# Scheduling edges that bind the casts and low parts of the MLP slabs' weights to the order of their jobs

## The chip, the cores and the metric

The kernel runs on one core of one Trainium2 chip. The metric is the device time of one execution in microseconds, taken as the median of several executions. Beside it there is a profiled execution, whose trace tells when each instruction of each engine ran. Engines are named as in the profile: PE is the matrix engine (TensorE), PEld its weight loads, DVE the vector engine, ACT the scalar engine, POOL the GpSimd engine, and SP the queue that issues most transfers.

## The reference

Two layers of a decoder trunk on 256 tokens of width 2048, in float32. What matters here is the MLP at the end of each layer, whose two weight matrices are 2048 x 8192 and 8192 x 2048:

```python
def squared_relu_mlp(h, w1, w2):
    z = jax.nn.relu(h @ w1)
    return (z * z) @ w2

for i in range(DEPTH):            # DEPTH = 2
    ...
    x = x + jnp.concatenate([token_out, mem_out], axis=-1) @ w_out[i]
    x = x + squared_relu_mlp(rms_norm(x, ffn_norm[i]), w_ff1[i], w_ff2[i])
```

The output is x, 1 x 256 x 2048.

## The kernel before

**Weights in two parts.** Every weight is loaded as float32 and split into a high part, which is a cast to the reduced type fp32r on ACT (line 176, `hi_ring`), and a low part, which is the weight minus its high part, on DVE (line 179, `lo_ring`). Each product is then three matmuls: high weight by high and low part of the activation, low weight by high part. Both rings have 6 slots of 512 columns. A slot is taken when the split is written down and given back when the matmuls that read it have been written down, so a cast can run only after the matmuls that read its slots before.

**Two streams of jobs share the rings.** `Feed` serves them in one written order, found in a dry run of the whole program (`Plan.close`):

- Plain quads ("N", m): four 128x128 blocks, one slot, cast from a tile `raw`. In the MLP they feed the up tiles (`up_tile`, products into `x_bank`).
- Slabs ("S", n, j): the second MLP matrix is multiplied in a scheme with seven products in place of eight on 2 x 2 blocks. Each layer has 56 slabs, numbered 0 to 55 in layer 0 and 56 to 111 in layer 1; a slab has four jobs. A job is written here as (n,j). Job 0 casts two slots from the tile `slab` (128x1024), job 1 one slot from `slab` (128x512), jobs 2 and 3 two slots each from the tile `room` (128x1024). Their products go into the banks `p`, with activations from `z` or from the sums `sit`.

**What a slab's jobs do beside the split** (`_prepare`). After job 0 the left half of the slab tile is no longer needed as it was, and POOL issues a transfer that adds other weights onto it (`add_right`, line 151); job 1 casts that sum. The same happens after job 2 for job 3, in `room`. Ahead of job 1 stands a step "K": an addition on DVE (line 201) that makes the first half of what job 2 casts; after job 2 another one (line 215) makes the half that job 3 adds onto.

**The order of the jobs** is written by hand (lines 1036 to 1041): for each p the jobs (p+1,0), (p,1), (p,2), (p-1,3). So around slab 50 the written order is

```
(51,0) K50 (50,1) (50,2) (49,3) | (52,0) K51 (51,1) (51,2) (50,3)
```

Between them stand up tiles and their quads; each job has a due time in units of up tiles (`tiles_at`). From slab 50 on the jobs stand further apart, since they are to last to the end of the second part of the MLP. `fill` writes the splits down three steps ahead of the job that reads them, if slots are free.

**After each up tile** its bank is copied by ACT to `room` (line 757), its halves are added (DVE, line 816), then come relu and square on ACT (820, 828), the cast to `z` (768) and its low part (772), the four differences for `sit` on DVE (789 to 792), and their cast and low part (797, 800).

**What sets the order on an engine.** Each engine runs its instructions in one order, fixed when the program is built. The builder starts from the written order and lets an instruction go ahead of an earlier one where, by its own estimate of times, the earlier one is not ready yet. `Feed.order` (line 153) adds an edge between two instructions that binds this choice alone and makes no semaphore. It is used before the change for a few pairs, among them each K step, which comes after the low part of the slab job written last (`last_low`, line 202).

Of the kernel before, what the change touches and what calls it, by code (L numbers as in the profile page):

```python
# [55 lines left out]
class Plan:  # L56
# [7 lines left out]
    def __init__(self):  # L64
        self.entries = []
        self.npos = 0
        self.jobs = []
        self.slabs = []
# [32 lines left out]
class Feed:  # L101


    def __init__(self, tc, wst, wpool, rows, plan, dry):
        self.tc, self.nc, self.wst, self.wpool, self.rows = tc, tc.nc, wst, wpool, rows
        self.plan, self.dry = plan, dry
        self.pos = 0
        self.slab_no = 0
        self.lp = self.pp = 0
        self.raw = {}  # L110
        self.split = {}
        self.second = None
        self.second_of = [None] * 3
        self.loads_ahead = LOADS
        self.behind = None
        self.cast_behind = []
        self.gate = None
        if not dry:
            self.hi = wpool.tile([P, SLOTS * 512], F32R, name="hi_ring")
            self.lo = wpool.tile([P, SLOTS * 512], F32R, name="lo_ring")  # L120
            self.busy = [False] * SLOTS
            self.at = 0
# [48 lines left out]
    def _split(self, job, src, n):  # L171
        a = self._slots(n)
        if a is None:
            return False
        hi, lo = self.hi[:, a * 512 : (a + n) * 512], self.lo[:, a * 512 : (a + n) * 512]
        self.last_cast = self.nc.scalar.copy(hi, src)  # L176
        if self.cast_behind:
            self.order(self.last_cast, self.cast_behind.pop())
        low = self.nc.vector.tensor_sub(lo, src, hi.bitcast(F32))  # L179
        if job[0] == "S":  # L180
            self.last_low = low
        if self.behind:
            self.order(low, self.behind)
            self.behind = None
        self.split[job] = (hi, lo, range(a, a + n))
        return True
# [1474 lines left out]
```

## Time and profile before

| | |
|---|---|
| median of 3 runs | 2005.38 us (2004.85 to 2005.83) |
| the profiled execution's own time | 2004.53 us |
| its span, first to last instruction | 2002.8 us |
| mean granted clock of PE | 0.999 |
| bytes moved by DMA | 420.10 MB, mean 210 GB/s |
| cast of a plain quad, ACT line 176 | 620 ns, 1001 of them |
| low part of a plain quad, DVE line 179 | 694 ns, 1001 of them |
| cast of a two-slot job from `room`, ACT | 1054 ns, 224 of them |
| low part of a two-slot job from `room`, DVE | 1222 ns, 224 of them |
| cast and low part from `slab` (two shapes), mean | 830 and 954 ns, 224 of each |
| accumulating transfers issued by POOL | 224, 256 KB each, median 5.8 us (`room`) and 6.6 us (`slab`) from issue to landing |

The profile's page gives each engine's busy time and the costliest groups of instructions. A row of the timeline has the start in us from the span's start, the duration, engine, line, operation, the names written and read with their shapes, the count of merged instructions, and in brackets the idle time of the engine before it with what ended that. The view of waits sums such idle times by the waiting group and its releaser. Matmuls are pipelined: consecutive ones overlap in the trace, so what counts is the step from start to start. Busy shares are averages over the whole span; what an edit is worth is read at the place where the engine that sets the end stands still.

### The profile page before, as it was taken

To read this page: it belongs to the slowest core of one execution; us is meant where nothing else is said; L and a number is where in the kernel's file an instruction comes from. 1 tells how busy PE (TensorE), PEld (TensorE's weight loads), DVE (VectorE), ACT (ScalarE), POOL (GpSimd) and SP (SyncE) were. 2 spreads that over 40 slices of the span, in tenths; PEclk is the share of its full clock that TensorE was granted. 3 is DMA by queue.
4 is the path that set the end of the run, shared out by engine and by line. 5 is a ranking of instruction groups with operands and counts; after the bars stand their busy time and mean duration, and the time that the engine had idled before them with its cause. 6 is when DMAs were issued, how large, how long until landed. Compare 5 with 4: busy or idle time off the path is not lost.

```text
span 2002.8 us, 32056 instructions
## 1 busy us (share of the span) xinstructions
PE 1993.9 (100%) x10534; PEld 1705.1 (85%) x10534; DVE 1716.2 (86%) x3089; ACT 1498.4 (75%) x2791; POOL 247.0 (12%) x291
## 2 busy tenths in 40 slices
PE   9999999999999999999999999999999999999999
PEld 8888888888888888888888888888888888888788
DVE  8888878889989899899765798878889899899887
ACT  7765577787887878778665699567787878878775
POOL 0001311111111111110000000311111111111110
PEclk9999999999999999999999999999999999999999
DMA  9566567888888888765675534567888888888774
GB/s 318 174 192 192 188 202 208 228 224 234 233 231 227 221 231 230 220 190 179 193 227 192 171 122 150 196 189 214 218 225 227 234 235 226 230 223 228 203 219 145
DMA packets 142727, 420.10 MB, mean 210 GB/s; under 512 B 16096, under 2 KB 18784, under 8 KB 142560
## 3 DMA queue, kind: packets, MB, share of 16 engines
q1 hardware_dynamic: 110160, 359.32, 55.4%
q0 software_dynamic: 32256, 58.73, 17.3%
q8 instruction: 82, 1.34, 0.3%
q14 instruction: 85, 0.70, 0.1%
q10 hardware_dynamic: 144, 0.01, 0.0%
HBM read 415.90 MB, written 2.10 MB: 209 GB/s over the span
## 4 chain that ended last, share of the span: by engine, by line
PE 82%; issue 14%; POOL 3%; DMA 1%; ACT 1%; DVE 1%; POOLq 0%; DVEq 0%; ACTq 0%
PE x_bank L430 19%; PE x_bank L432 9%; PE p L863 6%; PE p L865 6%; PE p L866 6%; PE wo L430 6%; PE wo L432 3%; PE u L430 2%; PE ff L430 2%; POOL room L151 1%; POOL slab L151 1%; PE u L432 1%; PE q L464 1%; PE q L466 1%; PE k L464 1%
## 5 line engine op out<-in xcount | busy, mean ns | idle before, releaser
L176 ACT CAST hi_ring<-raw 128x512 fp32r<-128x512 f32 x1001 | 613.2, 620 | 270.4 <-PE x_bank L430 67.8
L179 DVE TENSOR_TENSOR lo_ring<-raw,hi_ring 128x512 fp32r<-128x512 f32 x1001 | 685.7, 694 | 122.7 <-ACT hi_ring L176 107.2
L430 PE MATMUL x_bank<-fx,hi_ring 128*128 128x512 f32 x1952 | 611.1, 394 | 0.0
L432 PEld LDWEIGHTS x_bank<-fx,lo_ring 128*128 128x128 f32 x1952 | 367.0, 188 | 83.8
L432 PE MATMUL x_bank<-fx,lo_ring 128*128 128x256 f32 x1952 | 383.7, 278 | 0.0
L430 PEld LDWEIGHTS x_bank<-fx,hi_ring 128*128 128x128 f32 x1952 | 320.3, 189 | 24.4 <-ACT room L757 0.3
L176 ACT CAST hi_ring<-room 128x1024 fp32r<-128x1024 f32 x224 | 236.0, 1054 | 126.5 <-PE p L865 105.9
L179 DVE TENSOR_TENSOR lo_ring<-room,hi_ring 128x1024 fp32r<-128x1024 f32 x224 | 273.8, 1222 | 37.3 <-ACT hi_ring L176 28.5
L179 DVE TENSOR_TENSOR lo_ring<-slab,hi_ring 128x512 fp32r<-128x512 f32 (+1 forms) x224 | 213.7, 954 | 59.3 <-ACT hi_ring L176 58.5
L176 ACT CAST hi_ring<-slab 128x512 fp32r<-128x512 f32 (+1 forms) x224 | 186.0, 830 | 47.6 <-PE p L865 23.9
L863 PE MATMUL p<-hi_ring,sit 128*128 128x512 f32 x448 | 176.0, 393 | 1.6 <-ACT hi_ring L176 1.5
L866 PE MATMUL p<-lo_ring,sit 128*128 128x512 f32 x448 | 174.8, 390 | 1.8 <-DVE lo_ring L179 1.8
L865 PE MATMUL p<-hi_ring,sit 128*128 128x512 f32 x448 | 175.4, 391 | 0.0
L151 POOL DMA_DIRECT2D room<-in_w x112 | 96.9, 865 | 563.3 <-DVE lo_ring L179 451.0
L151 POOL DMA_DIRECT2D slab<-in_w x112 | 97.1, 867 | 527.9 <-DVE lo_ring L179 520.0
L430 PE MATMUL wo<-cat,hi_ring 128*128 128x512 f32 x512 | 161.8, 397 | 0.3 <-DVE rc L401 0.3
L863 PE MATMUL p<-hi_ring,z 128*128 128x512 f32 x336 | 132.1, 393 | 0.0
L865 PE MATMUL p<-hi_ring,z 128*128 128x512 f32 x336 | 131.2, 390 | 0.0
L866 PE MATMUL p<-lo_ring,z 128*128 128x512 f32 x336 | 130.8, 389 | 0.0
L432 PEld LDWEIGHTS wo<-cat,lo_ring 128*128 128x128 f32 x512 | 95.9, 188 | 22.0
L866 PEld LDWEIGHTS p<-lo_ring,sit 128*128 128x128 f32 x448 | 84.3, 188 | 21.3 <-DVE lo_ring L179 2.7
L432 PE MATMUL wo<-cat,lo_ring 128*128 128x256 f32 x512 | 101.5, 279 | 0.0
(375 smaller groups left out, 3369.4 us busy)
## 6 DMA issues: line engine op xcount, KB each, us to landing
raw<-in_w SPq DMA_DIRECT2D x500, 512.0 KB, 4.5
slab<-in_w SPq DMA_DIRECT2D x112, 512.0 KB, 4.7
room<-in_w SPq DMA_DIRECT2D x112, 256.0 KB, 4.7
slab<-in_w POOLq DMA_DIRECT2D x112, 256.0 KB, 6.6
room<-in_w POOLq DMA_DIRECT2D x112, 256.0 KB, 5.8
memraw<-in_mem SPq DMA_DIRECT2D x5, 512.0 KB, 4.5
resid<-in_x SPq DMA_DIRECT2D x8, 256.0 KB, 5.3
out_y<-resid SPq DMA_DIRECT2D x16, 128.0 KB, 1.9
```

The costliest lines, as they stand in the source:

```text
L151: self.nc.gpsimd.dma_start(t, self.wst[h, :, 0:512], accum_op=ALU.add)
L176: self.last_cast = self.nc.scalar.copy(hi, src)
L179: low = self.nc.vector.tensor_sub(lo, src, hi.bitcast(F32))
L430: nc.tensor.matmul(ps, hi, xs[:, k, :], start=first and c == 0, stop=False)
L432: nc.tensor.matmul(ps[:, T : 2 * T], lo, xs[:, k, 0:T], start=False, stop=last and c == len(ks) - 1,)
L464: nc.tensor.matmul(ps[t], x[t][1], hi, start=k == 0, stop=False)
L466: nc.tensor.matmul(ps[t], x[t][0], lo, start=False, stop=k == NK - 1)
L863: nc.tensor.matmul(ps, a[1], hi, start=new, stop=False, **again)
L865: nc.tensor.matmul(ps, a[0], hi, start=False, stop=False, **again)
L866: nc.tensor.matmul(ps, a[0], lo, start=False, stop=end, **again)
```

## The change

Each slab job's cast gets an edge to the cast of the slab job written before it, and each slab job's low part an edge to the low part before it. The first slab job has none. Plain quads get no edge, and nothing is added to, or taken from, the instructions themselves.

```diff
@@ -114,6 +114,7 @@
         self.loads_ahead = LOADS
         self.behind = None
         self.cast_behind = []
+        self.last_s = self.last_low = None
         self.gate = None
@@ -178,7 +179,10 @@
             self.order(self.last_cast, self.cast_behind.pop())
         low = self.nc.vector.tensor_sub(lo, src, hi.bitcast(F32))
         if job[0] == "S":
-            self.last_low = low
+            if self.last_low is not None:
+                self.order(self.last_cast, self.last_s.ins.name)
+                self.order(low, self.last_low.ins.name)
+            self.last_s, self.last_low = self.last_cast, low
         if self.behind:
             self.order(low, self.behind)
             self.behind = None
```

## The prediction

> **What bounds the kernel now.** I read the page first, then the waits summed by engine, then the timeline around the longest of them.
>
> ```profile
> span 2002.8 us, 32056 instructions
> ...
> PE 1993.9 (100%) x10534; PEld 1705.1 (85%) x10534; DVE 1716.2 (86%) x3089; ACT 1498.4 (75%) x2791; POOL 247.0 (12%) x291
> ```
>
> TensorE has work in the array for all but 8.9 us, so a change to the casts (ACT) and low parts (DVE) can only pay where TensorE waits for them. The view of waits, for PE alone (total us, times, longest), says where:
>
> ```profile
> PE p L866 <- DVE lo_ring L179: 1.8, 2, 0.9
> PE p L863 <- ACT hi_ring L176: 1.5, 1, 1.5
> PE warm L371 <- PEq L1634: 0.8, 1, 0.8
> PE st_mq L625 <- DVE mq_y L326: 0.3, 1, 0.3
> PE wo L430 <- DVE rc L401: 0.3, 1, 0.3
> ```
>
> 3.3 of these 4.7 us are waits of slab products (p) for a high or low part of their weights. The same view for ACT holds one row in which a cast waits for a slab's transfer:
>
> ```profile
> ACT hi_ring L176 <- DMA slab<-in_w: 8.8, 2, 5.1
> ```
>
> Two times, 3.7 and 5.1 us. The first is in layer 0; rows of the timeline (start, duration, idle before in brackets), thinned:
>
> ```profile
> 814.61 0.86 POOL L151 DMA_DIRECT2D slab<-in_w  x1 [2.62 <-DVE lo_ring L179]
> ...
> 816.00 0.62 ACT L176 CAST hi_ring<-slab 128x512 fp32r<-128x512 f32 x1
> ...
> 816.64 0.42 DVE L816 TENSOR_TENSOR room<-room 128x256 f32<-128x256 f32 x1
> ...
> 817.58 0.68 DVE L201 TENSOR_TENSOR room<-slab,room 128x512 f32<-128x512 f32 x1
> ...
> 818.67 0.63 PE L430 MATMUL x_bank<-fx,hi_ring 128*128 128x512 f32 x2
> ...
> 820.31 0.62 ACT L176 CAST hi_ring<-slab 128x512 fp32r<-128x512 f32 x1 [3.69 <-DMA slab<-in_w]
> ...
> 820.84 0.41 ACT L820 ACTIVATE room<-room 128x256 f32<-128x256 f32 x1
> ...
> 822.04 1.04 ACT L176 CAST hi_ring<-room 128x1024 fp32r<-128x1024 f32 x1
> ...
> 822.62 0.39 PE L866 MATMUL p<-lo_ring,sit 128*128 128x512 f32 x1
> ...
> 823.14 0.50 PE L863 MATMUL p<-hi_ring,sit 128*128 128x512 f32 x1
> ...
> 823.52 1.22 DVE L179 TENSOR_TENSOR lo_ring<-room,hi_ring 128x1024 fp32r<-128x1024 f32 x1
> ...
> 824.79 0.50 PE L866 MATMUL p<-lo_ring,sit 128*128 128x512 f32 x1 [0.92 <-DVE lo_ring L179]
> ...
> 825.13 0.39 PE L863 MATMUL p<-hi_ring,sit 128*128 128x512 f32 x1
> ...
> 826.20 1.05 ACT L176 CAST hi_ring<-room 128x1024 fp32r<-128x1024 f32 x1
> ```
>
> The shapes tell the jobs apart: job 0 casts 128x1024 from slab, job 1 128x512 from slab, jobs 2 and 3 128x1024 from room. The code writes ..., (50,1), (50,2), (49,3), (52,0), (51,1), .... The trace has slab 512 (816.00), slab 512 (820.31), room (822.04), room (826.20), slab 1024 (830.09, below): the cast of job (51,1) runs ahead of three casts written before it. It reads the half to which POOL's transfer of 814.61 adds, so ACT stands until that lands at 820.3, and behind it in ACT's queue stand relu, square and z cast (from 820.84) and the cast of (50,2), which TensorE needs next. Comparing written with run order over all 448 slab casts and 448 low parts, this place and its twin one layer later are the only inversions among them. The twin:
>
> ```profile
> 1892.25 0.62 ACT L176 CAST hi_ring<-slab 128x512 fp32r<-128x512 f32 x1 [5.10 <-DMA slab<-in_w]
> ...
> 1893.17 0.39 PE L866 MATMUL p<-lo_ring,sit 128*128 128x512 f32 x1
> 1895.07 0.50 PE L863 MATMUL p<-hi_ring,sit 128*128 128x512 f32 x1 [1.51 <-ACT hi_ring L176]
> ...
> 1896.73 0.53 PE L866 MATMUL p<-lo_ring,sit 128*128 128x512 f32 x1 [0.92 <-DVE lo_ring L179]
> 1897.06 0.62 PE L863 MATMUL p<-hi_ring,sit 128*128 128x512 f32 x1
> ```
>
> **The change part by part.** Of the 447 edges of each kind, those between neighbours that already stand in order move nothing: all but two. These two put the casts and low parts of (51,1) and (107,1) behind those of (52,0) and (108,0). No instruction, byte or semaphore is added.
>
> *What goes.* The undisturbed step between slab products is 0.225 us (834.25 to 834.70 below is two steps). Layer 0: 822.62 to 825.13 is four steps, 2.51 - 0.90 = 1.61 us lost. Layer 1: 1893.17 to 1897.06, 3.89 - 0.90 = 2.99 us. Then the windows (PE busy and count, PEld, DVE, ACT, POOL, granted clock, DMA share, GB/s):
>
> ```profile
> 825.13:827.11 1.98, 1.98 (x11) 1.48 (x9) 1.98 (x4) 1.98 (x4) 0.77 (x1) 1.00 0.50 33
> 1893.17:1897.06 3.89, 1.46 (x5) 0.59 (x4) 3.17 (x7) 3.28 (x7) 0.09 (x1) 1.00 0.00 0
> 1897.06:1900.47 3.41, 3.41 (x10) 2.75 (x9) 3.41 (x7) 2.34 (x5) 0.77 (x1) 0.50 0.46 122
> ```
>
> After the longer stall the granted clock is 0.50 for 3.41 us; the same stretch of the program took 1.98 us in layer 0 at 1.00, so 1.43 us more. Together 1.61 + 2.99 + 1.43 = 6.03 us.
>
> [...]
>
> *Does (50,2) come in time without it?* Its addend (L201) is done at 818.26. Its two ring slots, worked out from the ring's order, were last read by the matmuls of 818.67 and the low ones right behind: free at 819.30 and 819.53. Relu, square and z cast need the add of 816.64, done at 817.06, and 1.2 us of ACT (820.84 to 822.04): done at 818.3. So its cast runs 819.34 to 820.4 and its low part (1.22) to 821.6. TensorE wants them at 822.85 and 823.30: 2.4 and 1.7 us to spare. In layer 1 the spacing is the same. POOL's next accumulating transfer (after that low part) and SP's loads go earlier with it; both queues keep their order.
>
> *What (51,1) costs in its new place.* Its cast (0.62) and low part (0.68) now follow (52,0):
>
> ```profile
> 830.09 1.05 ACT L176 CAST hi_ring<-slab 128x1024 fp32r<-128x1024 f32 x1
> 831.05 1.14 ACT L176 CAST hi_ring<-raw 128x512 fp32r<-128x512 f32 x2
> 832.85 0.62 ACT L176 CAST hi_ring<-raw 128x512 fp32r<-128x512 f32 x1 [0.66 <-PE x_bank L430]
> ...
> 831.18 1.23 DVE L179 TENSOR_TENSOR lo_ring<-slab,hi_ring 128x1024 fp32r<-128x1024 f32 x1 [0.41 <-ACT hi_ring L176]
> 832.32 0.68 DVE L201 TENSOR_TENSOR room<-slab,room 128x512 f32<-128x512 f32 x1
> 832.92 2.49 DVE L179 TENSOR_TENSOR lo_ring<-raw,hi_ring 128x512 fp32r<-128x512 f32 x4
> ...
> 834.25 0.39 PE L863 MATMUL p<-hi_ring,sit 128*128 128x512 f32 x1
> ...
> 834.70 0.39 PE L866 MATMUL p<-lo_ring,sit 128*128 128x512 f32 x1
> ...
> 1903.48 1.05 ACT L176 CAST hi_ring<-slab 128x1024 fp32r<-128x1024 f32 x1 [1.52 <-PE x_bank L430]
> ```
>
> By its slot, (51,1) is first read at 834.25 (high) and 834.70 (low). The cast of (52,0) waits for TensorE to leave its slots (the last row, its twin in layer 1, tells it), so this stretch keeps its spacing and moves earlier as a whole. Placed right after (52,0), the cast ends at 831.8; the low part, behind the sum of L201, ends at 833.7, 1.0 us early. Queued behind them are the casts and low parts of two plain quads; on ACT the 0.66 us of idle before 832.85 takes the 0.62. If the builder puts all four plain low parts ahead, it ends at 836.0, 1.3 us late. So 0 to 1.3 us a layer; I take 0, because (51,1) is written ahead of those four quads. Its transfer landed at 820.3 and can't bind. DVE has the room:
>
> ```profile
> 818.86:840.00 21.14, 20.09 (x105) 16.44 (x105) 17.17 (x31) 15.84 (x28) 2.60 (x3) 1.00 0.69 199
> ```
>
> 17.17 us of DVE work (third pair) in 21.14, or in 19.53 without the 1.61: 88%.
>
> *Sum.* 2004.53 for the profiled execution less 6.03 is 1998.50. The median of the runs stands 0.85 above that execution, so 1999.35, call it **1999.4**. Were all of the 0.85 stall too, 1998.5; were 0.5 us of stall left at each place, 2000.4.
>
> **The rivals.**
> [...]
> - *A new wait at the new place:* (51,1) comes late by up to 1.3 us a layer, 1999.4 + 2.6 = 2002.0. For it: DVE's four low parts in a row at 832.92; against it: written order and 1.0 us to spare.
> - *Another reader of an accumulating transfer steps forward, slower:* the builder fills ACT's freed 0.62 us, its later choices shift, and some other job 1 or 3 is put ahead of plain casts before its transfer lands. Slab edges don't bind plain casts. Layers are built alike, so there would be two such stalls; at layer 1's price, 2.99 + 1.43 = 4.42 each, 1999.4 + 8.8 = 2008.2. It decides for slower once a stall costs more than 3.0 us; at layer 0's 1.61 it stays a gain. Against it: the row of ACT's waits for slab transfers counts only these two in 224 casts, and ACT at 75% finds its order again soon.
> - *The edges don't change what TensorE waits for*, because (50,2) is held by something the rows hide: 2005.4.
>
> **How the numbers follow.** Forecast 0.72; half clock stays 0.06; new wait 0.09; another reader 0.07; no effect 0.06. The likeliest alone spans 1998.5 to 2000.4. With the first two rivals the range is 1998.0 to 2002.0, which leaves out the last two and a little of the first. A measurement of this kernel tells 0.2%, 4.0 us, from no change, so faster means under 2001.4: 0.72 + 0.06 + half of 0.09, 0.82. Slower, above 2009.4: half of 0.07, 0.04. The rest, 0.14, is the same.
>
> **What would show it.** Right: ACT's waits for slab transfers are gone; the p rows are gone from PE's waits or down to tenths; the granted clock is 1.00 throughout the former 1897 to 1900; between the casts of (50,1) and (50,2) stands no second slab 512 cast; span 1996.8. Wrong: a p or x_bank row of PE waits over 1 us anywhere, above all at the first products with (51,1), or a new wait of ACT for slab or room transfers.

## The result, and the profile after

The changed kernel takes 1998.05 us (median of 6 runs, 1997.90 to 1998.52) against 2005.12 us (6 runs, 2004.04 to 2005.83): a ratio of 0.9966, 95% interval 0.9953 to 0.9978. The forecast was 1999.4 in a range of 1998.0 to 2002.0; the time lies 0.05 us above its lower edge. The profiled execution took 1997.90 us. The runs of the changed kernel lie within 0.6 us of each other, those of the kernel before within 1.8 (within 2.8 to 5.2 in the three larger sets of 15, 18 and 27 runs that were taken beside the experiments).

The page's span, and its chain of work that ended last, by engine, for the kernel before and after:

```profile
PE 82%; issue 14%; POOL 3%; DMA 1%; ACT 1%; DVE 1%; POOLq 0%; DVEq 0%; ACTq 0%
```

```profile
span 1996.1 us, 32052 instructions
...
PE 99%; ACT 0%; DVE 0%; issue 0%
```

The chain led through POOL's transfers before; now it is TensorE nearly from end to end. Matmuls, casts and low parts are as many as before; the four instructions fewer (32052 against 32056) are semaphore waits of ACT and DVE. The waits of PE after (total us, times, longest):

```profile
PE warm L375 <- PEq L1638: 0.8, 1, 0.8
PE st_mq L629 <- DVE mq_y L330: 0.3, 1, 0.3
PE wo L434 <- DVE rc L405: 0.3, 1, 0.3
```

The two rows of slab products are gone; the other three stand as they stood. ACT's waits hold no row for a slab's transfer any more. The timeline of layer 0 after, thinned (lines are 1 to 4 higher than before):

```profile
815.73 0.63 ACT L177 CAST hi_ring<-slab 128x512 fp32r<-128x512 f32 x1
816.88 0.42 ACT L824 ACTIVATE room<-room 128x256 f32<-128x256 f32 x1 [0.53 <-DVE room L820]
...
819.07 1.05 ACT L177 CAST hi_ring<-room 128x1024 fp32r<-128x1024 f32 x1 [0.88 <-PE x_bank L434]
...
828.08 1.57 ACT L177 CAST hi_ring<-slab 128x1024 fp32r<-128x1024 f32 x2 [1.53 <-PE x_bank L434]
829.55 1.90 ACT L177 CAST hi_ring<-raw 128x512 fp32r<-128x512 f32 x3
...
820.15 1.23 DVE L180 TENSOR_TENSOR lo_ring<-room,hi_ring 128x1024 fp32r<-128x1024 f32 x1 [0.37 <-ACT hi_ring L177]
...
830.90 0.69 DVE L180 TENSOR_TENSOR lo_ring<-slab,hi_ring 128x512 fp32r<-128x512 f32 x1
...
822.58 0.39 PE L867 MATMUL p<-hi_ring,sit 128*128 128x512 f32 x1
822.80 0.39 PE L869 MATMUL p<-hi_ring,sit 128*128 128x512 f32 x1
823.03 0.39 PE L870 MATMUL p<-lo_ring,sit 128*128 128x512 f32 x1
...
832.23 0.39 PE L867 MATMUL p<-hi_ring,sit 128*128 128x512 f32 x1
...
832.68 0.39 PE L870 MATMUL p<-lo_ring,sit 128*128 128x512 f32 x1
```

After the cast of (50,1) at 815.73 comes the relu, then the cast of (50,2) at 819.07, which now waits for TensorE to leave its slots and not for a transfer. TensorE steps through the products of (50,2) at 0.22 to 0.23 us each. The row of 828.08 merges two casts: (52,0), and right behind it (51,1).

How much each place gave is read from one and the same piece of the program, from the low product of (50,1) to the x_bank matmul behind the products of (49,3), as windows (span of the window; PE, PEld, DVE, ACT, POOL busy; granted clock; DMA share; GB/s). Before:

```profile
822.62:831.49 8.87, 7.82 (x38) 5.86 (x37) 8.23 (x15) 7.13 (x13) 0.86 (x1) 1.00 0.58 149
1893.17:1904.90 11.73, 9.30 (x39) 7.16 (x37) 8.99 (x17) 8.49 (x16) 0.86 (x1) 0.85 0.53 168
```

After:

```profile
822.35:829.48 7.13, 7.13 (x39) 6.09 (x38) 5.06 (x10) 5.14 (x10) 0.18 (x1) 1.00 0.92 282
1891.13:1898.27 7.14, 7.14 (x38) 6.09 (x37) 5.05 (x10) 5.14 (x10) 0.18 (x1) 1.00 0.94 286
```

8.87 - 7.13 = 1.74 us in layer 0 and 11.73 - 7.14 = 4.59 us in layer 1, 6.33 in all. Another 0.27 us was there before either place (822.62 against 822.35). It arises in the first 8 us of the span and comes and goes with the execution, not with the change: the same matmul starts at 822.32 in another trace of the kernel before (`before_again`) and at 822.90 in a kernel without either stall (`no_transfer`). The two profiled executions differ by 2004.53 - 1997.90 = 6.63 us.

### The profile page after: what moved, and what is told of

It is laid out like the page before. It is cut to its first block, busy times and chain, and to the rows that moved or that the text cites. A ratio compares the mean times of both kernels' runs of the same rounds, so it can differ in the third digit from the quotient of the medians.

```text
span 1996.1 us, 32052 instructions
## 1 busy us (share of the span) xinstructions
PE 1990.8 (100%) x10534; PEld 1704.1 (85%) x10534; DVE 1716.3 (86%) x3089; ACT 1497.9 (75%) x2791; POOL 246.5 (12%) x291
## 4 chain that ended last, share of the span: by engine, by line
PE 99%; ACT 0%; DVE 0%; issue 0%
PE x_bank L434 25%; PE x_bank L436 12%; PE p L867 9%; PE p L869 9%; PE p L870 9%; PE wo L434 6%; PE wo L436 3%; PE u L434 2%; PE ff L434 2%; PE u L436 1%; PE q L468 1%; PE q L470 1%; PE k L468 1%; PE k L469 1%; PE q L469 1%; PE v L469 1%
## 5 line engine op out<-in xcount | busy, mean ns | idle before, releaser
L177 ACT CAST hi_ring<-room 128x1024 fp32r<-128x1024 f32 x224 | 236.0, 1053 | 128.1 <-PE p L869 107.4
```

## The experiments

The theory: what costs is the landing of one accumulating transfer in each layer, which a cast that ran ahead waits for at the head of ACT's queue; and TensorE's idle time there brings on the half clock. Rivals: the early place costs by itself; the order on DVE matters as much; the many edges help in other places; the half clock has another cause. In the diffs, lines of the changed kernel that stay are not shown, nor are lines that only set a name up.

**Two edges in place of 894** (`two_edges`).

```diff
         if job[0] == "S":
-            if self.last_low is not None:
-                self.order(self.last_cast, self.last_s.ins.name)
-                self.order(low, self.last_low.ins.name)
+            if job[1:] in ((51, 1), (107, 1)):
+                self.order(self.last_cast, self.last_s.ins.name)
```

> Two edges in all: the cast of (51,1) behind that of (52,0), and the cast of (107,1) behind that of (108,0). Theory: the whole gain, 6.6 to 7.1 us, about 1998.1, since the low parts follow their casts by themselves and the other edges bind what stands in order. Rival (the many edges hold other places together): less than the whole.

1998.01 us (5 runs, 1997.90 to 1998.49), ratio to before 0.9964 (0.9950 to 0.9978). The whole gain. In the traces the order of instructions on ACT, DVE and POOL is the one of the changed kernel, so the other 892 edges do nothing, and the low parts follow their casts.

**Edges for one layer alone** (`layer0_only`, `layer1_only`).

```diff
-            if self.last_low is not None:
+            if self.last_low is not None and job[1] < 56:      # layer1_only: >= 56
```

> The edges are made for slabs 0 to 55 alone, so layer 0 runs as in the changed kernel and layer 1 as before. Theory (each place has its own price): 1.6 to 1.8 us less than before, about 2003.4; in the trace ACT's waits for slab transfers count one, 5 to 7 us after POOL's issue, in layer 1, and the clock still falls to 0.50 after it. Rival (the gain is of the edges as a whole, or of some other place that they shift): half of 6.6, or nothing.

> The edges are made for slabs 56 to 111 alone. Theory: 4.4 to 4.8 us less than before, about 2000.5, made up of about 3.0 us of stall and 1.4 to 1.6 us of half clock; the stall of layer 0 stays at 1.6 us. This and the run with layer 0 alone add up to the whole gain, 6.4 to 6.6. Rival (half each): 3.3.

Layer 0 alone: 2001.92 us against 2004.82 (27 runs), ratio 0.9985 (0.9976 to 0.9994), so 1.2 to 4.8 us less. Layer 1 alone: 2000.10 us, ratio 0.9979 (0.9970 to 0.9987), 2.6 to 6.0 us less. The medians' 2.9 and 4.7 us are unequal as expected and add up to 7.6, a little over the whole; the first is over the 1.6 to 1.8 expected. The mean granted clock of each run tells why. In the traces it is 1.000 where there was no half clock, 0.999 where that lasted 3.41 us and 0.998 where it lasted 6.83 us (below). Of the 27 runs of before, 20 stand under 1.000, ten of these at 0.998 or 0.997; of the 11 of layer 0 alone five do, all at 0.999. So the medians differ by half clock too, and not by the stall of layer 0 alone. Among the runs at 1.000 the medians are 2003.45 us (before, 7 runs), 2001.57 (layer 0 alone, 6) and 2000.10 (layer 1 alone, 9): 1.9 and 3.4 us less, together 5.2, against 5.4 for the changed kernel's 1998.05. In the traces the untouched place is there as before, first that of `layer0_only` (wait in layer 1), then that of `layer1_only` (wait in layer 0):

```profile
ACT hi_ring L177 <- DMA slab<-in_w: 5.2, 1, 5.2
```

```profile
ACT hi_ring L177 <- DMA slab<-in_w: 4.2, 1, 4.2
```

In one point the first trace was not as expected. TensorE's timeline in layer 1, and the window behind the stall:

```profile
1891.35 0.39 PE L870 MATMUL p<-lo_ring,sit 128*128 128x512 f32 x1
1893.35 0.50 PE L867 MATMUL p<-hi_ring,sit 128*128 128x512 f32 x1 [1.61 <-ACT hi_ring L177]
...
1895.00 0.50 PE L870 MATMUL p<-lo_ring,sit 128*128 128x512 f32 x1 [0.92 <-DVE lo_ring L180]
```

```profile
1895.40:1900.00 4.60, 4.60 (x26) 3.79 (x25) 4.43 (x9) 3.48 (x8) 0.71 (x1) 1.00 0.68 158
```

The stall is as long as in the first trace of before (1.61 + 0.92 us against 1.51 + 0.92), yet the clock stayed at 1.00. So a stall of this length does not always bring the half clock, and in an execution without it layer 1 costs 3.2 us, not 4.6.

**The transfers left out** (`no_transfer`): the kernel before, without the two accumulating transfers that the early casts wait for.

```diff
         if p[2] == 0:
-            self.add_right(p[1], ra[:, 0:512])
+            if p[1] not in (51, 107):
+                self.add_right(p[1], ra[:, 0:512])
```

> No edges, and the order as before, with the cast of (51,1) and of (107,1) ahead of three others; left out are the two accumulating transfers that these two casts wait for, so the left halves of these two slabs lack an addend. Theory (what costs is the landing that the early cast waits for, not its place): as the changed kernel, 6 to 7 us less than before, about 1998.4, with no wait of ACT for slab transfers. Rival (the place costs by itself, because the cast and low part of 1.3 us stand ahead of more urgent ones): 2003 to 2005.

1997.93 us (5 runs, 1997.90 to 1998.48), ratio 0.9967 (0.9954 to 0.9979). ACT's order is that of the kernel before, with (51,1) still ahead; the row merges its cast with that of (50,1), without a wait between them, and so its slot is free by then:

```profile
816.28 1.18 ACT L177 CAST hi_ring<-slab 128x512 fp32r<-128x512 f32 x2
```

The two pieces of the program above take 7.13 and 7.14 us, no excess at all. The place of the cast costs nothing; the landing it waits for costs everything.

**Edges between low parts alone** (`lows_only`).

```diff
             if self.last_low is not None:
-                self.order(self.last_cast, self.last_s.ins.name)
                 self.order(low, self.last_low.ins.name)
```

> Only the edges between low parts are made; the cast of (51,1) still runs ahead on ACT, its low part goes behind that of (52,0). Theory (ACT's queue is what holds TensorE): the wait of 3.7 to 5.1 us on ACT stays, the low part of (50,2) starts 0.4 us earlier in each layer, in all 0.8 us less than before, about 2004.3. Rival (the order on DVE matters as much): 2 to 3 us less.

2003.58 us, ratio 0.9993 (0.9984 to 1.0002), which alone would not tell 0.8 us from nothing. The trace does; the waits of PE and of ACT:

```profile
PE p L866 <- ACT hi_ring L177: 1.9, 2, 1.7
PE p L869 <- DVE lo_ring L180: 1.1, 2, 0.5
```

```profile
ACT hi_ring L177 <- DMA slab<-in_w: 9.0, 2, 5.3
```

ACT's waits stay, the wait for the low part falls from 0.92 to 0.5 us at each place, 0.4 as expected. The order on DVE is worth about an eighth of the whole.

**Idle time filled with work** (`keep_busy`, then `keep_busy2`): in the kernel before, seven matmuls with a block of zeros (`zero`, made once early in the program), ahead of the first product of (106,2).

```diff
             def run(j):
                 hi, lo = feed.job(n, j)
+                if n == 106 and j == 2:
+                    for _ in range(7):
+                        nc.tensor.matmul(
+                            banks[3][0:64, :], zero, xs[:, 0, :], start=False, stop=False,
+                            **(dict(skip_group_check=True) if back[3] else {}),
+                        )
```

> The kernel before, with seven more matmuls on a block of zeros (they add nothing) put into TensorE's order in layer 1, right ahead of the first product of (106,2), where it stands still for 1.5 us; they take about 7 x 0.225 = 1.6 us of that idle time. Theory (the half clock is the stall's): TensorE is idle for about 0.9 us only, the clock stays at 1.00, and though work is added the time falls by the 1.4 us of half clock, to about 2003.7. Rival (the half clock comes from something else, or from the start of the wait): the clock falls to 0.50 as before, time 2005.1 or a little over.

2004.68 us, ratio 0.9998 (0.9989 to 1.0007): no gain, where 2003.7 was expected. The clock did as expected: 1.00 in the trace, and a mean of 1.000 in 10 of the 11 runs, against 3 of the 15 of before beside them. But the added work also changed the builder's choice on ACT: a relu and a square came ahead of the cast of (105,3), and TensorE met a new wait of some 0.5 us for its low part. So the time of this run says nothing of what the half clock costs. The second one holds the order of before with an edge:

```diff
+            if job[1:] == (105, 3):
+                self.hold = self.last_cast.ins.name
...
                 one = nc.scalar.activation(y[:, 0:T], y[:, 0:T], AF.Relu)
+                if feed.hold and not dry:
+                    feed.order(one, feed.hold)
+                    feed.hold = None
```

> As the run with seven idle-time matmuls, but with one more edge that keeps the order on ACT and DVE as it was before the change (in the first such run the builder had put a relu and a square ahead of the cast of (105,3), and TensorE met a new wait of 0.5 us for its low part). Theory (idle time of TensorE in layer 1 brings the half clock, in some executions none, in others one or two windows of 3.4 us): the clock stays at 1.00, the stall stays as long, the runs lie closer together than those of before and their median 1 to 1.5 us lower, about 2003.4, near the lowest runs of before (2002.8). Rival (idle time is not what brings it): runs spread from 2002.8 to 2008 as before, with the same median.

TensorE's timeline in layer 1:

```profile
1893.72 1.78 PE L907 MATMUL p<-fx,zero 128*64 128x512 f32 x7
1895.58 0.50 PE L871 MATMUL p<-hi_ring,sit 128*128 128x512 f32 x1
...
1897.24 0.50 PE L874 MATMUL p<-lo_ring,sit 128*128 128x512 f32 x1 [0.92 <-DVE lo_ring L180]
1897.58 0.40 PE L871 MATMUL p<-hi_ring,sit 128*128 128x512 f32 x1
1897.81 0.39 PE L873 MATMUL p<-hi_ring,sit 128*128 128x512 f32 x1
```

The seven fit into the idle time, the product of (106,2) starts when it would have anyway, and the steps behind it are 0.23 us, at a granted clock of 1.00 (1897.58 to 1901). The 11 runs lie between 2002.66 and 2004.08, median 2003.52; the 18 of before beside them between 2003.16 and 2005.95, median 2005.30, thirteen of them above the highest of this kernel. The ratio, 0.9993 (0.9984 to 1.0002), just reaches 1, so the times alone do not close it. The clock does: all 11 runs have a mean of 1.000, against 4 of the 18 of before, while the order on ACT and DVE is that of before. So it is TensorE's idle time that brings the half clock in layer 1.

**The same seven matmuls where nothing is idle** (`after_fill`): put into the changed kernel at the same place.

> The changed kernel with the same seven matmuls on zeros at the same place, where there is no idle time any more. Theory: they cost their full 7 x 0.225 = 1.6 us, plus a tenth or two: about 1999.6, with a narrow spread as in the changed kernel. Rival (there is hidden slack left at that place): under 1998.6.

1999.61 us (8 runs, 1999.49 to 2000.14), ratio to before 0.9974 (0.9964 to 0.9984). That is 1.6 us over the changed kernel's 1998.05, and the trace shows the seven from 1891.76 to 1893.38, 1.62 us, with no gap on either side:

```profile
1891.76 1.78 PE L911 MATMUL p<-fx,zero 128*64 128x512 f32 x7
1893.38 0.39 PE L875 MATMUL p<-hi_ring,sit 128*128 128x512 f32 x1
```

Work that was free in the stall costs its full length once the stall is gone; no hidden slack is left there.

**The kernel before, twice more** (`before_again`, `before_look3`), no edit.

> The kernel before once more, for a second trace of it. Theory: how long the early cast waits depends on when its transfer lands, which is not the same in each execution, so the two stalls differ by some tenths of a us to a us from those of the first trace, and the half clock may come in both layers, in one, or in none; the changed kernel has no such wait, and its runs lie closer together. Rival: the same stalls to 0.1 us.

> The kernel before, a third trace. Theory: the two stalls end when the accumulating transfer lands, so they differ from those of the two other traces by tenths of a us; slow clock comes as none, one or two windows of 3.4 us after the stall of layer 1.

2005.91 and 2003.71 us. The granted clock behind the stall of layer 1, first trace and second:

```profile
1895.71:1902.54 6.83, 6.38 (x16) 4.76 (x17) 6.60 (x12) 5.35 (x10) 0.86 (x1) 0.50 0.51 117
```

```profile
1897.20:1904.00 6.80, 6.61 (x34) 5.52 (x35) 6.17 (x12) 5.62 (x11) 0.86 (x1) 1.00 0.75 201
```

Half clock for 6.83 us in the one, none in the other. In the one it starts inside the stall, at the first product behind a wait of 1.96 us. The excess at the two places, each as the length of the piece of program above less the 7.13 or 7.14 us of the changed kernel:

| trace of before | layer 0 | layer 1 | half clock | its time | time less both |
|---|---|---|---|---|---|
| first | 1.74 | 4.59 | 3.41 us | 2004.53 | 1998.20 |
| `before_again` | 2.21 | 5.84 | 6.83 us | 2005.91 | 1997.86 |
| `before_look3` | 2.16 | 3.57 | none | 2003.71 | 1997.98 |

What is left in the last column is the changed kernel's median to 0.2 us, in all three; 0.27 of the first row is the difference at the start. The stalls end when the transfer lands. In layer 1, POOL's issue to landing took 7.03, 7.48 and 7.49 us in the three traces, and TensorE's wait for the high part, against the 0.225 us step, was 1.68, 2.12 and 2.13 us: the same 0.45 more. A warning on reading: in these two traces the view gave the wait of the early cast to another engine,

```profile
1892.91 0.62 ACT L176 CAST hi_ring<-slab 128x512 fp32r<-128x512 f32 x1 [5.55 <-PE x_bank L430]
```

though the matmuls that had read its slot were done over 5 us earlier (in `no_transfer` the same cast runs at once, without a wait); what came just before 1892.91 was the landing, 1885.34 + 7.49 = 1892.83. A wait is best checked against what the instruction reads.

## Why the prediction was right, point by point

- *Where the time is lost.* Right. Two places, one in each layer, held all of it: the windows of the changed kernel, the two single-layer runs and the table show nothing elsewhere but the 0.27 us at the start, which is not the change's.
- *What goes: 1.61 + 2.99 + 1.43 = 6.03 us.* 1.74 and 4.59 us measured between the profiled executions. The terms were 0.13 and 0.17 us short, since the first two were read over four steps and left out a longer step just behind them (825.83 to 826.40, 0.57 us where the changed kernel has 0.46), and the third was measured against layer 0, which has that longer step too. The third term, the half clock, had the right cause (`keep_busy2`), but it is no constant: none, 3.41 or 6.83 us of it came in different executions, where I took the one trace for all of them. That this trace showed the middle one of the three was luck.
- *The median: 1999.4 forecast, 1998.05 measured.* The forecast set 0.85 us of spread between the profiled execution and the median aside as belonging to the machine. That is the mis-sized step: the spread was the stall's own. It went away with it (1997.90 profiled, 1998.05 median, 0.15 apart in place of 0.85), which makes 0.70 of the difference of 1.35 us; the rest is the 0.30 us by which the two places were short, the 0.27 at the start, and rounding. The prediction named this case, 1998.5, and did not choose it. Even so the time lies below the 1998.5 to 2000.4 that it called the likeliest, in the last half us of the range, for which it names no term: that it lies inside the range is luck in part, and the mechanism is what the runs bear out.
- *(50,2) in time.* Forecast: cast at 819.34, low part done at 821.6. Measured: 819.07 and 821.38, both with the 0.27 us that this execution was ahead: the same times.
- *(51,1) in its new place.* Forecast to cost nothing, low part 1.0 us ahead of its reader. It ends at 831.59, its reader starts at 832.68: 1.1 us. The builder chose the written order, as assumed.
- *The rivals.* The half clock stays without a stall (0.06): the five traces without either stall or with idle time filled in layer 1 (the changed kernel, `two_edges`, `no_transfer`, `after_fill`, `keep_busy2`) have a mean clock of 1.000, as have all 24 runs of the first four of these; the changed kernel's trace has 0.50 only at the end of the span (1995.4 to 1996.1), behind TensorE's last matmul. A new wait or another early reader: none. No effect: refuted.

## What to carry to other kernels

An instruction that waited for a transfer, 3.7 and 5.1 us here, cost nothing by its place (7.13 and 7.14 us without the transfers, as in the changed kernel); what cost, 1.74 and 4.59 us with the half clock, was the work held up behind it in its engine's queue. Where a builder orders a queue by its own estimates, look for the one instruction that was let ahead with a wait of several us before it, and bind that one. And the runs of the kernel before, with two waits on the path that ended at a transfer's landing, spread by 1.8 to 5.2 us, those of the changed kernel by 0.6: such a spread can be a sign of such a wait, and then it goes with the wait.

## What the runs showed of the hardware

The half clock came in lengths of 3.41 us (twice, the first trace and `lows_only`) and 6.83 us (`before_again`), that is once and twice the same length, or not at all (`layer0_only`, `before_look3`), at stalls of layer 1 with 2.2 to 2.9 us of idle time in all. One run of before at a clock of 0.997 (2008.12 us) points to still more of it, but has no trace. In the seven traces with the stall of layer 0, with 0.7 to 1.6 us idle, the half clock did not come behind that one. It seems to come there at times: with this stall alone (`layer1_only`) two of the 11 runs, 2002.40 and 2002.51 us, stand at a clock of 0.999, and the other nine, at 1.000, take 2000.90 or less. No trace shows it. What let it come at 2.2 us of idle time (`lows_only`) and stay away at 2.9 (`before_look3`) no run shows.
